# Both feed-forward products of an encoder block by Strassen's seven block products

## The chip, the cores and the metric

One core of a Trainium2 chip runs the whole program. The metric is the device time of one execution in microseconds; three runs of the kernel before took 2787.19, 2792.93 and 2794.11 us. TensorE (PE) multiplies, PEld is its weight load; VectorE (DVE), ScalarE (ACT) and GpSimd (POOL) work on elements; SyncE (SP) and POOL issue DMAs.

## The reference

An encoder block on x of 2048 tokens and width 1024, all float32. Two branches (a gated MLP that mixes tokens in chunks of 128, and neighbourhood attention) are merged by sigmoid gates and projected; then comes the part that the change touches:

```
x  = x + merged @ w_out                                    # 1024 x 1024
h2 = rms_norm(x, norm2_g)                                  # per token
x  = x + square(relu(h2 @ w_ff1)) @ w_ff2                  # 1024 -> 4096 -> 1024
```

The norm's factor of a token is positive and constant over the width, so both kernels multiply by it after the first product.

## The kernel before

Everything is held transposed: tiles have 128 features on the partitions and 512 tokens along the free axis. Each float32 operand is split into a rounded part (hi, an ACT copy to float32r) and what that leaves (lo, a DVE subtraction that reads both from SBUF); a product of a 128x128 weight tile and a 128x512 activation tile is three matmuls, hi hi, hi lo and lo hi (`gemm`, line 141). `split` (lines 108 and 109) does it for weights.

The program computes the input projections for both halves of 1024 tokens, then attention with the gates' products in between (line 600 on), then for each half `merge` for two blocks of 512 tokens (line 646), `out_proj` (line 677) and `ffn` (line 694). `merge` loads both branches (`load_y`, line 633, issued by POOL), gates and weights, multiplies, and leaves 8 tiles of merged features in parts in SBUF. `out_proj` adds the product to x (line 688), makes the scaled parts of the norm's input (lines 256 and 257) and the sums of squares.

`ffn` takes 256 columns of w_ff1 at a time, 16 chunks. `up` gives for each of two column tiles and two token blocks one accumulation group of 8 x 3 matmuls, then relu times the norm's factor (DVE, line 703), square (ACT, line 704) and the split into parts (lines 706 and 707), which stay in SBUF. `down` multiplies two such rows by 256 rows of w_ff2: for each of 8 output tiles and two token blocks 2 x 3 matmuls, added to x by DVE from the PSUM bank (line 717). `down` of a chunk is written ahead of `up` of the chunk two later.

SBUF is cut into slots of 4 KB per partition: 5 for raw weights, 12 for their parts, 29 for activations. PSUM has 8 banks of 128x512: 3 for products ("mm"), 2 for scores ("s"), 2 for transposes and one more. Dependencies and semaphores are set by a tile framework. It also orders each engine's instructions: a planner goes through them with expected durations, and an engine takes the first in the text that is ready by then. On the chip each engine keeps to the order planned. `keep_in_program_order` pins an instruction behind the one before it in the text.

Of the kernel before, what the change touches and what calls it, by code (L numbers as in the profile page):

```python
# [32 lines left out]
NRAW, NW, NACT = 5, 12, 29  # L33
# [4 lines left out]
# Queries go in tiles of 8 rows and 16 columns. First key row and key rows of a block of query rows;  # L38
# first key column, key columns and kind of bias table of a block of query columns.
# [18 lines left out]

class Block:
    """The encoder block; one method for each part of it."""  # L60

    def __init__(self, ctx, tc, a):
        self.tc, self.nc, self.a = tc, tc.nc, a
        self.waiting = []
        pool = lambda name, bufs, **k: ctx.enter_context(tc.tile_pool(name=name, bufs=bufs, **k))
        self.slots = pool("slots", 1)
        self.half = pool("half", 5)
# [4 lines left out]
        self.ybp = pool("ybp", 1)  # L72
# [26 lines left out]
    def split(self, shape, src, name, pool=False):  # L99
        """float32 tile -> its float32r part and what that leaves, which is a float32r too."""  # L100
# [11 lines left out]
    def load_raw(self, w, c0, ncol, nkt, name):  # L112
        """Columns c0.. of a weight, all of its rows."""
# [8 lines left out]
    def split_w(self, raws, name, pool=False):  # L122
        """A function (kt, part) -> [128, columns]."""
# [12 lines left out]
    def gemm(self, out, pairs):  # L136
        """pairs: (stationary parts, moving parts) along the contraction."""
# [6 lines left out]
    def later(self, fn, n=1):  # L144
        """fn's instructions come after the next n products', so that TensorE needn't wait for their inputs."""
# [10 lines left out]
    def rsqrt(self, r, m, n):  # L156
        """r = m ** -0.5, the square root's table refined by a Newton step."""
# [85 lines left out]
    def load_x(self, tok):  # L243
        """x transposed, 512 tokens: [kt] -> [128, 512]."""
# [8 lines left out]
    def parts(self, x, g, name):  # L253
        """x times the norm's gain, in parts."""
# [5 lines left out]
    def squares(self, acc, x, first):  # L260
        """acc: sums of squares over the rows of x tiles, by partition."""
# [8 lines left out]
    def rms(self, acc, n=1):  # L270
        """Each token's factor of the RMS norm: a column for each 128 tokens, and along the free axis on all
        partitions. To come after the next n + 1 products."""
# [3 lines left out]
        def columns():  # L276
# [7 lines left out]
            b = self.h512(name="rs_b").rearrange("p (t q) -> p t q", t=4)  # L284
            nc.vector.tensor_copy(b, col.rearrange("p (t o) -> p t o", o=1).broadcast_to([P, 4, P]))
            self.later(lambda: turn(b))

        def turn(b):
# [3 lines left out]
            self.nc.scalar.copy(row, pt)  # L292

# [3 lines left out]
    def norm(self, xs, n):  # L297
        """The RMS norm's factors of 512 tokens."""
# [6 lines left out]
    def tok_gemm(self, w, hT, t):  # L305
        """[128 tokens of tile t, 512 columns]"""
# [5 lines left out]
    def feat_gemm(self, w, m, X, nk=8):  # L312
        """[128 columns (the m-th of w), 512 tokens]"""
# [60 lines left out]
    def mix(self, h, t, v, uT):  # L374
        """Mixes a chunk's tokens and multiplies by u."""
# [101 lines left out]
    def att_load(self, pair, rb):  # L477
        """Keys (parts on the two partition halves), queries (doubled) and values of 8 rows of queries."""
# [29 lines left out]
    def att_queries(self, unit):  # L508
        """The queries, a tile's after another's."""
# [12 lines left out]
    def att_scores(self, unit, bias, cb):  # L522
        """Softmax of two heads' scores."""
# [59 lines left out]
    def att_out(self, po, o, c2):  # L583
        """Two column blocks' outputs, in parts and in the tokens' order."""
# [48 lines left out]
    def load_y(self, src, tok):  # L633
        ys = []
        for k in range(4):
            t = self.slot([2, 512], F32R, "y")
            self.nc.gpsimd.dma_start(t, src[:, :, k, tok : tok + 512])
            ys.append(t)
        return ys

    def load_gates(self, tok, m):
        g = self.slot([2, 512], F32, "gates")
        self.nc.sync.dma_start(g, self.gt.rearrange("(i m p) t -> m p i t", i=2, p=P)[m, :, :, tok : tok + 512])
        return g

    def merge(self, tok, out):
        """out: the merged branches, transposed and in parts; in pieces to be called in turn."""
        nc, a = self.nc, self.a
        load = lambda c: [self.load_wk(a[n][0], c * 256, 256, 4, n) for n in ("w_o_a", "w_o_b")] if c < 4 else None
# [5 lines left out]
        gs = [self.load_gates(tok, m) for m in range(2)]  # L655
        for c in range(4):
            (wa, wb), nxt = nxt, load(c + 1)
            for mm in range(2):
                m = 2 * c + mm
                g = gs.pop(0)  # L660
# [5 lines left out]
                pa = self.feat_gemm(wa, mm, ya, 4)  # L666
                pb = self.feat_gemm(wb, mm, yb, 4)
# [3 lines left out]
                o = self.slot([2, 512], F32R, "mg")  # L671
                nc.scalar.copy(o[:, 0], g[:, 0])
                nc.vector.tensor_tensor(o[:, 1], g[:, 0], o[:, 0].bitcast(F32), ALU.subtract)
                out.append(o)
                yield

    def out_proj(self, x1, mg):
        """Adds to x1, and its norm: parts and factors."""
        a = self.a
        h2T = []  # L680
        acc = self.h512(name="acc")
# [143 lines left out]
```

## Time and profile before

| | |
|---|---|
| median of three runs | 2792.93 us (2787.19 to 2794.11) |
| span of the profiled execution | 2789.8 us |
| PE busy | 2755.4 us (99%), 12996 matmuls |
| DVE, ACT, POOL busy | 1441.9, 791.2, 177.2 us |
| DMA | 327.30 MB, mean 117 GB/s |

The page of the profile gives the span of the profiled execution, from its first instruction to its last, and no time of its own for what lies around that; the median of the runs stands 3.1 us above the span. A row of a group of instructions reads: line, engine, operation, tile written <- tiles read, shapes, count | busy us, mean ns of one | idle us of the engine before them <- what ended that. Matmuls are pipelined, so a matmul's mean length (389 ns) is longer than the distance from one to the next.

### The profile page before, as it was taken

What the parts mean: (1) busy time and instruction counts of PE and PEld (TensorE: products, weight loads), DVE (VectorE), ACT (ScalarE), POOL (GpSimd) and SP (SyncE); (2) the same over time, 40 slices, a digit from 0 to 9 for tenths busy, and PEclk for the clock granted to TensorE, in tenths of its full rate; (3) what the DMA queues carried; (4) which work ended last, traced back from release to release, by engine and by line L of the source; (5) the groups of instructions that cost most, each with busy time, mean ns of one, the idle gap of its engine ahead of it and who ended that gap; (6) DMA issues with size and microseconds to landing.
All of it is one profiled execution on the core that took longest, in us unless ns stands there. A gap on an engine that the chain in (4) does not pass through costs nothing.

```text
span 2789.8 us, 33783 instructions
## 1 busy us (share of the span) xinstructions
PE 2755.4 (99%) x12996; PEld 2262.3 (81%) x12996; DVE 1441.9 (52%) x2604; ACT 791.2 (28%) x1336; POOL 177.2 (6%) x232
## 2 busy tenths in 40 slices
PE   8999999999999999999999999999999999999999
PEld 7888888887777777888888888887788888888887
DVE  6555225556656576545445444455654445454454
ACT  6333225232333342432222212222442211212111
POOL 0006500002212100000000000000000000000000
PEclk9999999999999999999999999999999999999999
DMA  6458832456888886421111111147631111111101
GB/s 189 116 134 219 242 107 71 135 134 176 226 233 230 235 271 223 146 81 46 46 46 46 61 46 46 46 129 234 202 102 59 46 46 46 54 53 46 46 23 61
DMA packets 262225, 327.30 MB, mean 117 GB/s; under 512 B 24429, under 2 KB 177428, under 8 KB 262064
## 3 DMA queue, kind: packets, MB, share of 16 engines
q1 hardware_dynamic: 239072, 280.53, 33.9%
q0 software_dynamic: 21952, 44.60, 5.9%
q8 instruction: 103, 1.69, 0.3%
q14 instruction: 58, 0.48, 0.1%
q10 hardware_dynamic: 1040, 0.00, 0.0%
HBM read 245.77 MB, written 79.25 MB: 117 GB/s over the span
## 4 chain that ended last, share of the span: by engine, by line
PE 94%; DVE 3%; DMA 2%; ACT 1%; issue 1%; SPq 0%; DVEq 0%; ACTq 0%
PE fg L141 76%; PE tg L141 11%; PE pv L575 2%; PE pTp L562 2%; PE s L533 2%; DMA gates<-gt 1%; PE mix L379 1%; DVE p L549 0%; PE qT L420 0%; DMA wg<-in_w_in_dram 0%; DVE acc L268 0%; PE ms L280 0%; DMA w_o_a<-in_w_o_a_dram 0%; DMA wk<-in_w_in_dram 0%; DVE p L540 0%
## 5 line engine op out<-in xcount | busy, mean ns | idle before, releaser
L141 PE MATMUL fg<-h2T,w_hi 128*128 128x512 f32 x2048 | 630.9, 389 | 0.0
L141 PE MATMUL fg<-aT,w_hi 128*128 128x512 f32 x2048 | 630.8, 389 | 0.0
L717 DVE TENSOR_TENSOR x<-fg,x 128x512 f32<-128x512 f32 x512 | 353.4, 690 | 251.1 <-PE fg L141 250.1
L141 PEld LDWEIGHTS fg<-aT,w_hi 128*128 128x128 f32 x2048 | 384.4, 188 | 80.5 <-DVE aT L707 0.7
L141 PEld LDWEIGHTS fg<-h2T,w_hi 128*128 128x128 f32 x2048 | 384.1, 188 | 79.6
L141 PE MATMUL fg<-h2T,w_lo 128*128 128x512 f32 x1024 | 398.4, 389 | 0.0
L141 PE MATMUL fg<-aT,w_lo 128*128 128x512 f32 x1024 | 398.4, 389 | 0.0
L141 PE MATMUL fg<-hT,wg_hi 128*128 128x512 f32 x1024 | 330.2, 398 | 0.0
L703 DVE SCALAR_TENSOR_TENSOR relu<-fg,rs_row 128x512 f32<-128x512 f32 x128 | 88.5, 691 | 305.1 <-PE fg L141 305.1
L108 ACT CAST w_hi<-w 128x1024 fp32r<-128x1024 f32 x128 | 134.1, 1052 | 343.9 <-PE fg L141 343.9
L141 PEld LDWEIGHTS fg<-hT,wg_hi 128*128 128x128 f32 x1024 | 191.5, 189 | 44.3 <-issue 7.4
L141 PEld LDWEIGHTS fg<-h2T,w_lo 128*128 128x128 f32 x1024 | 192.2, 188 | 40.0
L141 PEld LDWEIGHTS fg<-aT,w_lo 128*128 128x128 f32 x1024 | 192.2, 188 | 39.8
L141 PE MATMUL fg<-hT,wg_lo 128*128 128x512 f32 x512 | 202.7, 396 | 0.0
L109 DVE TENSOR_TENSOR w_lo<-w,w_hi 128x1024 fp32r<-128x1024 f32 x128 | 156.0, 1221 | 87.7 <-ACT w_hi L108 87.6
L704 ACT ACTIVATE relu<-relu 128x512 f32<-128x512 f32 x128 | 80.8, 631 | 420.6 <-DVE relu L703 420.6
L141 PE MATMUL fg<-mg,wo_hi 128*128 128x512 f32 x512 | 158.1, 390 | 0.0
L706 ACT CAST aT<-relu 128x512 fp32r<-128x512 f32 x128 | 79.5, 621 | 252.2 <-PE fg L141 249.1
L462 DVE TENSOR_TENSOR g<-fg,rs_row 128x512 f32<-128x512 f32 x64 | 44.1, 690 | 177.6 <-PE fg L141 174.2
L707 DVE TENSOR_TENSOR aT<-relu,aT 128x512 fp32r<-128x512 f32 x128 | 88.1, 688 | 76.8 <-ACT aT L706 76.8
L543 ACT ACTIVATE p<-p,nmx 128x480 f32<-128x480 f32 (+5 forms) x128 | 76.6, 600 | 149.8 <-DVE nmx L540 149.2
L141 PEld LDWEIGHTS fg<-hT,wg_lo 128*128 128x128 f32 x512 | 96.8, 189 | 19.7 <-issue 1.0
(166 smaller groups left out, 3525.0 us busy)
## 6 DMA issues: line engine op xcount, KB each, us to landing
w<-in_w_ff_dram SPq DMA_DIRECT2D x128, 512.0 KB
x<-in_xT_dram SPq DMA_DIRECT2D x32, 512.0 KB
wg<-in_w_in_dram SPq DMA_DIRECT2D x32, 512.0 KB
gt<-g SPq DMA_DIRECT2D x64, 256.0 KB
qn<-qs SPq DMA_DIRECT2D x64, 256.0 KB
gates<-gt SPq DMA_DIRECT2D x32, 512.0 KB
wo<-in_w_out_dram SPq DMA_DIRECT2D x32, 512.0 KB
ya<-ya SPq DMA_DIRECT2D x16, 512.0 KB
```

The source lines that it names most:

```text
L108: nc.scalar.copy(hi, src)
L109: nc.vector.tensor_tensor(lo, src, hi.bitcast(F32), ALU.subtract)
L141: self.nc.tensor.matmul(out, w[p], x[q], start=(i == 0 and j == 0), stop=(i == n - 1 and j == 2))
L533: nc.tensor.matmul(s.rearrange("p (r k) -> p r k", k=w), qt[hd][:, cb, l, :], kt[hd][:, :, k0 : k0 + w], start=(l == 0), stop=(l == 1),)
L543: nc.scalar.activation(p[:, hd], p[:, hd], AF.Exp, bias=nmx[:, hd : hd + 1], scale=-1.0, accum_out=sums[:, hd : hd + 1])
L562: nc.tensor.transpose(tp[: r * w, j // per, :], p[:, hd, j * w : (j + r) * w], self.ident)
L575: self.nc.tensor.matmul(po[hd * HD : (hd + 1) * HD, cb % 2 * P : (cb % 2 + 1) * P], unit[3][cb // 2][:m, cb % 2, j // per, hd * HD : (hd + ...
L703: nc.vector.scalar_tensor_tensor(r, pt, 0.0, rs[b][1], ALU.max, ALU.mult)
L704: nc.scalar.activation(r, r, AF.Square)
L706: nc.scalar.copy(o[:, 0], r)
L707: nc.vector.tensor_tensor(o[:, 1], r, o[:, 0].bitcast(F32), ALU.subtract)
L717: nc.vector.tensor_tensor(x, pt, x, ALU.add)
```

## The change

The feed-forward of a half is computed on 1024 tokens at once, and both its products as 2x2 blocks: two tiles of 128 columns by two blocks of 512 tokens by pairs of contraction tiles. In Winograd's form of Strassen's method four block sums on each side go in, seven block products are made instead of eight, and their sums come out. The sums over PSUM are partly made by letting a product go on accumulating in a bank after an earlier product in it has been read out.

POOL makes the four block sums of weights (`w_prep`) and of activations (`x_prep`); ACT and DVE then split each into parts. relu's squared result is stored whole to DRAM (`af`) and loaded again for the second product. There the contraction is visited in sliding groups: a visit (j, lo, hi) adds row pairs lo to hi-1 to output pair j; the 19 visits of a half have 1, 2, 3, then thirteen times 4, then 3, 2, 1 row pairs, so that each loaded pair serves four visits in a row and is then dropped. Preparation for the next step (`jobs`) is written between the seven products of the present one.

SBUF is shared out anew for the second part: 51 buffers of 4 KB that are taken from and given back to a list, on the memory of the old pools; a new buffer waits only for the tiles that it lies on. In the first half the merged tiles are stored to DRAM (`mg`) and loaded again. `load_y` issues from SP there. The attention and the input projections keep their code; comments and docstrings are gone.

```diff
+    def second_part(self):
+        self.part.close()
+        self.second = True
+        self.more = self.ctx.enter_context(self.tc.tile_pool(name="more", bufs=1, reuse_waits="tile"))
+        self.free = list(range(NBUF))
+    def take(self, shape, dt=F32, name="buf"):
+        i = self.free.pop(0)
+        return i, self.more.tile([P] + shape, dt, tag=f"b{i}", name=name)
...
+                if not self.second:
+                    nc.sync.dma_start(self.mg[tok // 512, m], o.bitcast(F32))
...
+    def w_prep(self, o):
+        n = o["n"]
+        r1, r2 = o["r1"][1], o["r2"][1]
+        o["t23"] = self.take([n, 2, P], F32, "w_s23")
+        s23 = o["t23"][1]
+        self.sub(s23[:, :, 1], r1[:, :, 0], r1[:, :, 1])
+        self.nc.gpsimd.tensor_tensor(r1[:, :, 1], r1[:, :, 1], r2[:, :, 1], ALU.add)
+        yield
+        o["t4"] = self.take([n, P], F32, "w_s4")
+        self.sub(s23[:, :, 0], r1[:, :, 1], r1[:, :, 0])
+        self.sub(o["t4"][1], r2[:, :, 0], s23[:, :, 0])
+        yield
+        self.parts_of(o, "r1", [n, 2, P])
+        yield
+        self.parts_of(o, "t23", [n, 2, P])
+        yield
+        self.parts_of_one(o, "t4", [n, P])
+        self.parts_of(o, "r2", [n, 2, P])
...
+    def x_prep(self, o):
+        r1, r2 = o["r1"][1], o["r2"][1]
+        o["t23"] = self.take([2, 512], F32, "x_t23")
+        t23 = o["t23"][1]
+        self.sub(t23[:, 1], r2[:, 1], r1[:, 1])
+        self.sub(r1[:, 1], r1[:, 1], r1[:, 0])
+        yield
+        o["t4"] = self.take([512], F32, "x_t4")
+        self.sub(t23[:, 0], r2[:, 1], r1[:, 1])
+        self.sub(o["t4"][1], r2[:, 0], t23[:, 0])
+        yield
...
+    def seven(self, w, xs, evac, jobs, done=()):
+        nc = self.nc
+        n = len(xs)
+        z, x, y = self.ps("z", "mm"), None, None
+        for i, p in enumerate((1, 5, 6, 3, 7, 2, 4)):
+            if p == 5:
+                x = self.ps("x", "s")
+            elif p == 2:
+                y = self.ps("y", "s")
+            out = {5: x, 3: x, 2: y}.get(p, z)
+            (wn, wi), (xn, xi) = self.W_AT[p], self.X_AT[p]
+            for k in range(n):
...
+                for j, (u, v) in enumerate(((0, 0), (0, 1), (1, 0))):
+                    nc.tensor.matmul(out, a[u], b[v], start=(p in (1, 5, 2) and k == 0 and j == 0), stop=(k == n - 1 and j == 2),
+                                     skip_group_check=p in (6, 3, 7, 4))
+            self.flush()
...
+            evac[p](out)
+            for _ in range(-(-len(jobs) // (7 - i))):
+                jobs.pop(0)()
...
+        def up_evac(c):
...
+            def finish(n, i, src):
+                t, v = e[n]
+                r = rs[i][1]
+                nc.vector.scalar_tensor_tensor(v[:, i], src, 0.0, r, ALU.max, ALU.mult)
+                nc.scalar.activation(v[:, i], v[:, i], AF.Square)
+                e[n, i] = True
+                if (n, 1 - i) in e:
+                    nc.sync.dma_start(self.af[2 * c + n, :, tok : tok + 1024].rearrange("p (b t) -> p b t", b=2), v)
+                    self.give(t)
...
+            return {1: copy(0, 0), 5: copy(1, 1), 6: copy(0, 1), 3: add(0, 1), 7: add(1, 1), 2: add(0, 0),
+                    4: lambda bank: finish(1, 0, bank)}
+        def down_evac(j):
...
+            return {1: add((0, 0)), 5: add((1, 1)), 6: add((0, 1)), 3: add((0, 1)), 7: add((1, 1)), 2: add((0, 0)), 4: add((1, 0))}
...
+        for c in range(NU):
+            nw = wl1(c + 1) if c + 1 < NU else wl2(0)
+            jobs = self.pieces(self.w_prep(nw))
+            self.seven(w, xs, up_evac(c), jobs, xs if c == NU - 1 else ())
+            w = nw
...
+        for j in x_new(0):
+            j()
+        for v, (j, lo, hi) in enumerate(visits):
...
+            self.seven(w, [win[k] for k in range(lo, hi)], down_evac(j), jobs, done)
```

In `seven`, `a` and `b` are the two parts of the weight and activation blocks that the product uses. Each add of `down_evac`, and the first operation of each add of `up_evac`, is a DVE addition of a PSUM bank to a tile in SBUF; `parts_of` is one ACT copy and one DVE subtraction of a whole 128x1024 buffer, `parts_of_one` of 128x512, `sub` a POOL subtraction. In `out_proj` the row pairs of x are scaled by ACT and prepared by `x_prep` in the second block's steps (`h2_jobs`).

## Rows read from the trace of the kernel before

**Rows 1.** The page: span, busy time by engine, granted clock in 40 slices.

```profile
span 2789.8 us, 33783 instructions
PE 2755.4 (99%) x12996; PEld 2262.3 (81%) x12996; DVE 1441.9 (52%) x2604; ACT 791.2 (28%) x1336; POOL 177.2 (6%) x232
PEclk9999999999999999999999999999999999999999
```

**Rows 2.** Chain of waits, its longest pieces: start us, us, what.

```profile
1217.26 685.69 PE fg L141 x3024
...
2100.28 685.69 PE fg L141 x3024
```

**Rows 3.** Stretches: length, then engines' busy us, clock, DMA share, GB/s.

```profile
core 0: us, PE busy (x) PEld busy (x) DVE busy (x) ACT busy (x) POOL busy (x), PEclk, DMA share, GB/s
1000.00:1080.80 80.80, 78.85 (x447) 62.78 (x445) 60.47 (x135) 34.52 (x71) 5.61 (x8) 1.00 0.87 268
...
1217.30:1902.90 685.60, 685.60 (x3025) 567.43 (x3024) 329.42 (x443) 146.34 (x197) 5.89 (x9) 1.00 0.20 62
1902.90:1963.90 61.00, 54.66 (x230) 44.34 (x228) 34.25 (x45) 21.92 (x31) 5.28 (x8) 0.94 0.73 225
```

**Rows 4.** Groups by line, whole span.

```profile
L717 DVE TENSOR_TENSOR x<-fg,x 128x512 f32<-128x512 f32 x512 | 353.4, 690 | 251.1 <-PE fg L141 250.1
...
L109 DVE TENSOR_TENSOR w_lo<-w,w_hi 128x1024 fp32r<-128x1024 f32 x128 | 156.0, 1221 | 87.7 <-ACT w_hi L108 87.6
L108 ACT CAST w_hi<-w 128x1024 fp32r<-128x1024 f32 x128 | 134.1, 1052 | 343.9 <-PE fg L141 343.9
...
L707 DVE TENSOR_TENSOR aT<-relu,aT 128x512 fp32r<-128x512 f32 x128 | 88.1, 688 | 76.8 <-ACT aT L706 76.8
...
L704 ACT ACTIVATE relu<-relu 128x512 f32<-128x512 f32 x128 | 80.8, 631 | 420.6 <-DVE relu L703 420.6
...
L706 ACT CAST aT<-relu 128x512 fp32r<-128x512 f32 x128 | 79.5, 621 | 252.2 <-PE fg L141 249.1
...
L106 POOL TENSOR_TENSOR wg_lo<-wg,wg_hi 128x1024 fp32r<-128x1024 f32 x16 | 38.4, 2398 | 50.2 <-PE tg L141 38.0 <-PE fg L141 9.1 <-POOL wg_hi L105 1.7
...
L256 ACT ACTIVATE h2T<-x,g 128x512 fp32r<-128x512 f32 x32 | 23.1, 723 | 77.5 <-DVE x L688 52.0 <-PE fg L141 18.8 <-issue 6.7
```

**Rows 5.** Timeline of POOL, its shorter additions: start us, us, instruction.

```profile
232.07 0.96 POOL L218 TENSOR_TENSOR tbt<-tbt,cmask 128x360 f32<-128x360 f32 x1 [0.70 <-DMA tbt<-sk]
...
268.80 2.10 POOL L218 TENSOR_TENSOR tbt<-tbt,cmask 128x480 f32<-128x480 f32 x1 [1.76 <-DMA tbt<-sk]
```

**Rows 6.** Timeline of POOL, 657 to 666 us.

```profile
658.79 2.37 POOL L106 TENSOR_TENSOR wg_lo<-wg,wg_hi 128x1024 fp32r<-128x1024 f32 x1
661.11 1.03 POOL L105 CAST wg_hi<-wg 128x1024 fp32r<-128x1024 f32 x1
...
664.50 1.04 POOL L105 CAST wg_hi<-wg 128x1024 fp32r<-128x1024 f32 x1
```

**Rows 7.** Timeline of DVE in the same stretch.

```profile
658.98 2.21 DVE L165 TENSOR_SCALAR rsq_t<-rsq_t 128x8 f32<-128x8 f32 x1
661.22 0.94 DVE L166 TENSOR_TENSOR qrs<-qrs,rsq_t 128x8 f32<-128x8 f32 x1
...
664.62 0.69 DVE L408 TENSOR_TENSOR qn<-tg,qrs 128x512 f32<-128x512 f32 x1
```

**Rows 8.** Timeline of DVE around 269 us.

```profile
268.59 1.22 DVE L109 TENSOR_TENSOR wg_lo<-wg,wg_hi 128x1024 fp32r<-128x1024 f32 x1 [2.89 <-ACT wg_hi L108]
```

**Rows 9.** Timeline of SP's queue at the end of the first half.

```profile
1861.98 1.52 SPq L643 DMA_DIRECT2D gates<-gt  x3
...
1885.40 18.62 SPq L720 DMA_DIRECT2D out_dram<-x  x15
```

**Rows 10.** The y tiles' DMAs, from issue to landing.

```profile
DMA to landing us min/median/max: 4.1/6.7/10.9
```

**Rows 11.** Chain of waits, its last piece: start us, us, what.

```profile
2785.99 0.69 DVE x L717
```

More of the change, by code (lines that the diff above doesn't have):

```diff
@@ L83, in __init__, with first_part, give, new @@
         self.tb = [[d(f"tb{i}{j}", [NH, 8, 16, n * w]) for j, n in enumerate(KIND_N)] for i, w in enumerate(KIND_W)]
+        self.af = d("af", [FF // P, P, S])
+        self.mg = d("mg", [2, 8, P, 2, 512])
+    def first_part(self):
+        part = ExitStack()
+        pool = lambda name, bufs: part.enter_context(self.tc.tile_pool(name=name, bufs=bufs, reuse_waits="tile"))
+        self.slots = pool("slots", 1)
+        self.half = pool("half", 5)
+        self.ybp = pool("ybp", 1)
+        self.part = part
+    def second_part(self):
[6 more added lines that the diff above has]
+        return i, self.more.tile([P] + shape, dt, tag=f"b{i}", name=name)
+    def give(self, *ts):
+        self.free += [t for t in ts if t is not None]
+    def new(self, shape, dt, name, tag="act"):
+        return self.take(shape, dt, name) if self.second else (None, self.slot(shape, dt, name, tag))
     def slot(self, shape, dt=F32, name="slot", tag="act"):
@@ new lines, in pieces, with load_out @@
+    @staticmethod
+    def pieces(gen, n=5):
+        return [lambda: next(gen, None)] * n
+    def load_out(self, c):
+        own, ts = [], []
+        for r in range(2):
+            raw, rv = self.take([4, 256], F32, "wo")
+            src = self.a["w_out"][0][r * 512 : (r + 1) * 512, c * 256 : (c + 1) * 256]
+            self.nc.sync.dma_start(rv, src.rearrange("(k p) n -> p k n", p=P))
+            hi, lo = self.take([4, 256], F32R, "wo_hi"), self.take([4, 256], F32R, "wo_lo")
+            self.hilo(hi[1], lo[1], rv)
+            self.give(raw)
+            own += [hi[0], lo[0]]
+            ts.append((hi[1], lo[1]))
+        return own, lambda kt, hl: ts[kt // 4][hl][:, kt % 4]
@@ new lines, in load_merged, with out_proj @@
+    def load_merged(self, b):
+        out = []
+        for m in range(8):
+            t, v = self.take([2, 512], F32R, "mg")
+            self.nc.sync.dma_start(v.bitcast(F32), self.mg[b, m])
+            out.append((t, v))
+        return out
+    def out_proj(self, tok, mgs):
+        nc, a = self.nc, self.a
+        self.x1 = [self.take([2, 512], F32, "x1") for _ in range(8)]
+        for m in range(8):
+            nc.sync.dma_start(self.x1[m][1].rearrange("p b t -> p (b t)"), a["xT"][m * P : (m + 1) * P, tok : tok + 1024])
+        x1 = [x[1] for x in self.x1]
+        acc = self.take([2, 512], F32, "acc")
+        sq = self.take([2, 512], F32, "sq")
+        rs, xs, jobs = [], [], []
+        steps = [(b, c) for b in range(2) for c in range(4)]
+        nxt = self.load_out(0)
+        if not mgs:
+            mgs = [self.load_merged(0)]
+        for i, (b, c) in enumerate(steps):
+            (own, w), nxt = nxt, self.load_out(steps[i + 1][1]) if i < 7 else None
+            if i == 1 and len(mgs) < 2:
+                mgs.append(self.load_merged(1))
+            for mm in range(2):
+                m = 2 * c + mm
+                pt = self.feat_gemm(w, mm, [v for _, v in mgs[b]])
+                x = x1[m][:, b]
+                nc.vector.tensor_tensor(x, pt, x, ALU.add)
+                if m == 0:
+                    self.tc.keep_in_program_order(nc.scalar.activation(acc[1][:, b], x, AF.Square))
+                else:
+                    nc.scalar.activation(sq[1][:, m % 2], x, AF.Square)
+                    nc.vector.tensor_tensor(acc[1][:, b], acc[1][:, b], sq[1][:, m % 2], ALU.add)
+                for _ in range(min(3, len(jobs))):
+                    jobs.pop(0)()
+            self.give(*own)
+            if c == 3:
+                rs.append(self.rms(acc[1][:, b], 1))
+                self.give(*(t for t, _ in mgs[b]))
+            if b == 1:
+                jobs += self.h2_jobs(x1, c, xs)
+        self.give(sq[0])
+        for j in jobs:
+            j()
+        return xs, rs, acc[0]
```

261 lines of the change are left out of this document (176 added, 85 removed).

## The prediction

> **What bounds the kernel now.** I read the busy times first: TensorE (PE) is busy 2755.4 us of a span of 2789.8, VectorE (DVE) 1441.9, ScalarE (ACT) 791.2, GpSimd (POOL) 177.2, at a granted clock of nine tenths or more in all slices [rows 1]. Then the chain of waits: its two longest pieces are the two feed-forward halves, each 3024 matmuls in 685.69 us with nothing between them [rows 2], so 0.22675 us per 512-column matmul. The table of stretches says the same: PE busy 685.60 of 685.60 us there, DVE 329 (48%), the DMA engines 20%; only where a merge begins does the DMA come near its limit, 268 GB/s at a share of 0.87, and PE stands 2 to 6 us [rows 3]. So time goes with the number of matmuls, as long as nothing else fills up. The page's span is 2789.8 us and the median of the three runs 2792.93; the 3.1 us outside the span are added at the end as a constant.
>
> **What it removes.** Up, a chunk of 256 columns and 1024 tokens took 4 groups of 8 x 3 matmuls, 96; it now takes 7 block products of 4 x 3, 84, so 1344 per half instead of 1536. Down, a visit of n row pairs takes 7 x 3n = 21n, and the n of a half sum to 64: again 1344 instead of 1536. Per half 2688 instead of 3072; 768 matmuls fewer in all, 768 x 0.22675 = **174.1 us off** the path, since PE has no gaps to absorb it.
>
> **What it adds on the other engines.** A full up step and a full down visit (n = 4) now last 84 x 0.22675 = 19.05 us on PE. Per operand set, weights or activations, there are four POOL additions of 128x512 and four splits, three of 128x1024 and one of 128x512, each an ACT copy and a DVE subtraction. DVE: 3 x 1.221 + 0.688 = 4.35 us; ACT: 3 x 1.052 + 0.621 = 3.78 [rows 4]. A POOL addition of 512 elements is not in the trace; between 360 elements at 0.96 us [rows 5] and 1024 at 2.398 [rows 4] a straight line gives 1.29 us, so 5.2 per set (bounds 1.0 and 2.4 each).
> Up step: DVE 4.35 + 7 evictions x 0.69 = 9.2 of 19.05, ACT 3.78 + 3 copies + 4 squares at 0.63 = 8.2, POOL 5.2. All lie beside PE. A product that accumulates on a bank (third, fourth, fifth, seventh) waits for an eviction of 0.69 us while a whole other product (12 matmuls, 2.7 us) runs: covered. I take 0.1 us per step for 32 steps, **+3** (bounds 0 and 32).
> Down visit: two sets per visit, so DVE 8.7 + 7 x 0.69 = 13.5 (71%), ACT 7.6, POOL 10.3, DMA 2.1 MB, half of what the 268 GB/s of rows 3 move. relu's result adds 16.8 MB out and 16.8 in per half, 54 GB/s over some 620 us. Taken one by one every engine is hidden. Taken together they are not, and that is the main point of this forecast.
>
> **The port.** While POOL ran an addition of 2.37 us (658.79 to 661.16) [rows 6], an 8-element DVE instruction begun at 658.98 took 2.21 us, and a two-input one of 8 elements begun at 661.22 took 0.94, to the end of the POOL cast of 661.11 [rows 7]. In the other direction a POOL addition of 480 elements took 2.10 us where the line above gives 1.22: it began at 268.80, inside a DVE subtraction that ran from 268.59 to 269.81 [rows 5, 8]. So such pairs exclude each other for their whole length. But the DVE multiplication from PSUM at 664.62 took its usual 0.69 us inside the next POOL cast [rows 7]. The Trainium skill (GPSIMD Engine Reference, Specifications) says that the SBUF interfaces are shared with VectorE, with contention for DVE instructions in a 2-port mode or with two SBUF inputs; by that the splits are held and the evictions, which read a PSUM bank, are not, as these rows show on small instructions. By the rule a visit needs 19.0 us of the port, without it 13.5 of DVE, and the sum below would lose its two largest terms.
> From the rows: splits 8.7 + additions 10.3 = **19.0 us of exclusive work in a visit of 19.05**. The port becomes as full as PE, with two in-order queues on it. Nothing is lost if both always have work ready; if DVE stood for every addition, it would need 13.5 + 10.3 = 23.8. I take one addition's length, 1.29 us, per full visit, as a held split delays the eviction behind it in DVE's queue, and the product two places later waits for that bank. There are 12 such visits per half (the thirteenth prepares no activations): 24 x 1.29 = **+31** (bounds 0 and 24 x 4.75 = 114).
>
> **The ramp.** The first three visits of a half have n = 1, 2, 3: 126 matmuls, 28.6 us on PE. Before the fourth, four activation sets and weights of n = 1 to 4 must be prepared: 4 x (5.2 + 4.35) = 38.0, POOL 13.9 for the weights, splits 11.8 (the same lines at 128 to 512 elements), 63.7 us of port. The last up step leaves 19.05 - (4.35 + 3 x 0.69 + 5.2) = 7.5, and 5 us of it is due only inside the fourth visit. Left uncovered: 63.7 - 28.6 - 7.5 - 5 = 22.6 per half, **+46** for two (bounds 2 x 10, when loads come early enough for more of it to lie in the up steps, and 2 x 45, when DVE and POOL alternate and the first load waits for the last store). Here idle PE may also lose its clock: in the stretch with 6.3 us of idle time the granted clock was 0.94 of full, 7.3 us at the half level, worth up to 3.7 us [rows 3]; that is inside the bounds.
>
> **From output projection to up.** The last row pair is complete only at the end of the projection: eviction 0.69, scaling 1.05 to 1.45, two additions 2.6, copy 1.05, subtraction 1.22 [rows 4]: 6.8 us, against some 2.5 us of matmuls on the other three pairs and the norm's; 4.3 stand open, with 3.7 for the clock 8 per half, **+16** (bounds 4 and 24).
>
> **Starts of the halves.** First half: merged tiles go out to DRAM and come back (4.2 MB each way before the projection can finish a column), and the new buffers lie on the old pools' memory. At 268 GB/s [rows 3] the 8.4 MB are 31 us in a stretch whose DMA is full; the way back, 16 us, I count in full, **+16** (bounds 3, if merge matmuls hide it, and 35: x1, first weights and merged tiles, 9.4 MB, all after the last merge product). Second half: the y loads move from POOL's queue into SP's, with stores and weights ahead of them. The order there isn't that of the text: three gate loads at 1861.98 stand ahead of the fifteen stores from 1885.40 [rows 9], so part goes out early. One y load took 6.7 us to land [rows 10]. **+4** (bounds -6, the present idle gone, and +20: 5.2 MB at 268 GB/s). Within each merge, the mixed order and the weights are as before.
>
> **Tail.** The last visit has 4.76 us of PE against 7 evictions, 4.83, and the last store is 512 KB instead of 256; the final addition ends 3.1 us before the span does now [rows 1, 11]: **+3** (bounds 1 and 6).
>
> **Sum.** -174.1 + 3 + 31 + 46 + 16 + 16 + 4 + 3 = -55; 2789.8 - 55 + 3.1 = **2738 us**. With all lower bounds -152 (2641), with all upper +147 (2940).
>
> **Rivals.**
> A. *The port is no bound*: POOL's additions fall where DVE waits for PE, as 250.1 us of DVE's idle time before the present evictions is waiting for PE [rows 4]. Visits cost nothing, the ramp 20: losses 62, so 2681 us. Against it: 19.0 of 19.05 leaves no room for queueing.
> B. *DVE and POOL take turns*: each full visit takes 23.8 us because splits wait for additions and evictions wait behind splits; 114 + 90 for the ramp + 42 for the other terms = 246, **slower, 2865 us**. It decides from 22.6 us per full visit, (174 - 88)/24 = 3.6 over PE's 19.05, with the ramp as forecast. For it: rows 7, where DVE got through only between POOL instructions. Against it: evictions are not held, and 5.5 us of a visit DVE has nothing to do.
> C. *The transfers decide*: both starts at their upper bounds (35 and 20) and the projections at 24, everything else as forecast: losses 162, 2781 us, hardly any change. For it: DMA share 0.87 already. Against: planned order with early loads.
> D. *It does not do what it says*: the matmuls are fewer but slower than 0.22675, as accumulating groups wait for evictions in visits of n = 1 and 2, where a product is 0.7 to 1.4 us. Five such visits per half, at most 12 us in all beyond the ramp: 2750; it changes no sign.
>
> **Chances.** Forecast 0.41 (own range 2700 to 2775), A 0.27, B 0.15, C 0.14, D 0.03. Differences below 0.3%, 8 us, can't be told from none here. Faster: forecast, A, D and some of C, 0.75; same, from C, 0.06; slower, B and the rest of C, 0.19. The range takes in A and most of C and stops short of B: 2650 to 2830.
>
> **What will show it.** 5376 matmuls in the seven products, at a start-to-start of 0.227 in a full up step, which must last 19 to 19.2 us. In a full down visit I expect 20 to 21 us, DVE splits of 2 us and more wherever a POOL addition runs, and PE's idle time there put down to DVE. If splits keep 1.22 us beside additions, the port was wrong. Visits 0 to 2 should take about 50 us instead of 28.6, mostly waiting for DVE and POOL; a gap of 4 to 8 us should stand ahead of each first up step, and about 16 ahead of the first projection with DMA as the releaser. A full visit at 22.6 us or more would make the forecast wrong in sign; 19.1 would make it A.

## The result and the profile after

The changed kernel takes 2859.09 us (median; 2855.48 to 2865.75) against 2792.58 of the kernel before, a ratio of 1.0243 (95% interval 1.0228 to 1.0259). It is slower, where 2738 and faster were forecast. The page of the kernel after, span, busy times and granted clock, against [rows 1]:

```profile
span 2853.0 us, 33593 instructions
PE 2653.3 (93%) x12228; PEld 2154.5 (76%) x12228; DVE 1584.5 (56%) x2606; ACT 1008.8 (35%) x1600; POOL 776.1 (27%) x656
PEclk9999999999999998989999999999999999999999
```

The 768 matmuls are gone (12996 to 12228), PE's busy time fell by 102 us, and its share from 99% to 93%: PE now waits for some 200 us. The stretches of the first half, columns as in [rows 3] (start of the up steps, up steps, first visits, full down visits):

```profile
1231.00:1268.00 37.00, 18.77 (x68) 14.75 (x68) 24.37 (x25) 16.87 (x22) 19.77 (x13) 0.72 0.15 43
1275.00:1540.00 265.00, 265.00 (x1171) 219.41 (x1169) 126.02 (x154) 106.59 (x153) 74.59 (x59) 1.00 0.33 109
1564.40:1606.30 41.90, 33.66 (x128) 25.23 (x127) 41.70 (x43) 18.57 (x23) 33.65 (x20) 0.92 0.32 109
1606.30:1902.80 296.50, 253.06 (x1010) 203.59 (x1009) 170.62 (x184) 85.30 (x96) 136.21 (x97) 0.92 0.27 88
```

In the up steps PE is as full as in [rows 3]. In the full visits it is idle for 43 of 296.5 us at a granted clock of 0.92, yet DVE is busy only 58% of the time, POOL 46% and DMA 27%: no engine is full there. From the first matmul of each step to that of the next, the span's 63.2 us (2853.0 - 2789.8) fall to these places, against the terms of the forecast:

| place | measured | forecast |
|---|---|---|
| 768 matmuls fewer, at 0.22675 us each | -174.1 | -174.1 |
| 24 full down visits (24.7 and 24.4 us each, 19.05 of matmuls) | **+131.8** | +31 |
| output projection to up: 18.2 us without a product in each half, the first projection itself 4.0 longer, first up steps 26.3 and 24.7 | **+52.8** | +16 |
| ramp: first three visits 41.8 and 44.3 for 28.6, last up steps 23.3 and 21.6 | +35.8 | +46 |
| first product of the first output projection later | +21.5 | +16 |
| up steps 2 to 15, 19.04 us each | 0 | +3 |
| end visits, tail, start of the second half (the rest) | -4.6 | +7 |

What a full visit waits for is seen by setting one of PE's waits beside the other engines' queues. Timeline of PE, DVE, ACT and POOL of the kernel after (start us, us, instruction, idle time before it and what ended it):

```profile
1739.94 0.39 PE L838 MATMUL x<-r_hi,t_hl 128*128 128x512 f32 x1
1744.08 0.75 PE L838 MATMUL z<-t_hi 128*128 128x512 f32 x1 [3.75 <-DVE x L1000]
1744.63 0.63 PE L838 MATMUL z<-t_lo,t_hi 128*128 128x512 f32 x1
1745.06 0.63 PE L838 MATMUL z<-t_hi,t_lo 128*128 128x512 f32 x1
...
1747.60 0.40 PE L838 MATMUL z<-t_hi,t_lo 128*128 128x512 f32 x1
...
1732.21 0.69 DVE L1000 TENSOR_TENSOR x<-z,x 128x512 f32<-128x512 f32 x1 [2.03 <-PE z L838]
1734.93 0.69 DVE L1000 TENSOR_TENSOR x<-x,x 128x512 f32<-128x512 f32 x1 [2.03 <-PE x L838]
1739.88 1.35 DVE L746 TENSOR_TENSOR r_lo<-a_r,r_hi 128x1024 fp32r<-128x1024 f32 x1 [4.25 <-ACT r_hi L745]
1741.15 2.28 DVE L746 TENSOR_TENSOR r_lo<-w_r,r_hi 128x1024 fp32r<-128x1024 f32 x1
1743.35 0.68 DVE L1000 TENSOR_TENSOR x<-z,x 128x512 f32<-128x512 f32 x1
...
1738.79 1.05 ACT L745 CAST r_hi<-a_r 128x1024 fp32r<-128x1024 f32 x1 [13.34 <-POOL a_r L742]
...
1732.11 1.29 POOL L782 TENSOR_TENSOR w_r<-w_r,w_r 128x512 f32<-128x512 f32 x1 [1.28 <-DMA w_r<-in_w_ff_dram]
...
1737.47 1.29 POOL L742 TENSOR_TENSOR a_r<-a_r 128x512 f32<-128x512 f32 x1
...
1740.22 2.12 POOL L742 TENSOR_TENSOR x_t<-a_r,x_t 128x512 f32<-128x512 f32 x1
```

Read it from below. POOL makes the sums for the next visit one behind the other, 1.29 us each, so `a_r` is done at 1738.8. On DVE the splits of `a_r` and `w_r` stand ahead of the eviction of `z` (the matmul after the last one into `z` started at 1737.45). DVE idles 4.25 us at the head of its queue for `a_r`, then splits for 3.5 us, one of them held by the POOL addition of 1740.22, and only then evicts. In the text of `seven` this eviction comes first; the instruction order that was planned for DVE has it behind. An eviction that nothing holds starts 0.43 us after its last matmul has started (so in e2 below), which would be at 1737.65 here. It starts 5.7 us later: 2.2 us are DVE's idle time, 3.5 us the two splits, of which the hold makes about 1.1 (2.28 for 1.22). The product in between covers part of that. PE waits 3.75 us, and its next matmuls then start 0.43 us apart instead of 0.227, until 1747.60, at a granted clock of 0.52. Together 19.05 + 3.75 + 1.6 = 24.4 us. The waits of DVE and of PE in the full visits of the first half (us in total, times, longest):

```profile
DVE r_lo L746 <- ACT r_hi L745: 53.9, 14, 6.5
...
PE z L838 <- DVE x L1000: 39.6, 11, 4.0
```

Between output projection and up the same engines meet again. POOL, DVE and PE of the kernel after, second half:

```profile
2136.40 1.27 POOL L742 TENSOR_TENSOR x_t<-h_r,h_r 128x512 f32<-128x512 f32 x1 [4.89 <-ACT h_r L926]
...
2138.97 2.24 POOL L742 TENSOR_TENSOR w_s<-w_r 128x512 f32<-128x512 f32 x1
2141.17 2.24 POOL L742 TENSOR_TENSOR x_t<-h_r,h_r 128x512 f32<-128x512 f32 x1
...
2144.60 2.27 POOL L742 TENSOR_TENSOR x_t<-h_r,x_t 128x512 f32<-128x512 f32 x1
...
2138.24 4.05 DVE L746 TENSOR_TENSOR r_lo<-h_r,r_hi 128x1024 fp32r<-128x1024 f32 x2
...
2148.57 2.30 DVE L746 TENSOR_TENSOR r_lo<-w_r,r_hi 128x1024 fp32r<-128x1024 f32 x1
...
2148.52 0.80 PE L838 MATMUL z<-r_hi 128*128 128x512 f32 x1 [10.52 <-ACT r_hi L745]
```

The last output projection matmul started at 2130.3, the first up product at 2148.5. The first weights' sums stand among those of the last row pair on POOL, and additions of 1.29 us take 2.2 beside splits, splits of 1.22 us take 2.0 to 2.3 beside additions. This is the exclusion of [rows 6 to 8] on whole tiles, in both directions; the eviction of 1732.21, which reads a PSUM bank, took its usual 0.69 us inside the POOL addition of 1732.11. With the rule that the prediction quotes (the Trainium skill, GPSIMD Engine Reference, Specifications: contention for DVE instructions with two SBUF inputs) these rows agree: splits, which have two, are held, the eviction is not.

### The profile page after: what moved, and what is told of

The parts are those of the page before. It is cut to its first block, busy times and chain, and to the rows that moved or that the text cites. A ratio compares the mean times of both kernels' runs of the same rounds, so it can differ in the third digit from the quotient of the medians.

```text
span 2853.0 us, 33593 instructions
## 1 busy us (share of the span) xinstructions
PE 2653.3 (93%) x12228; PEld 2154.5 (76%) x12228; DVE 1584.5 (56%) x2606; ACT 1008.8 (35%) x1600; POOL 776.1 (27%) x656
## 4 chain that ended last, share of the span: by engine, by line
PE 71%; DVE 8%; DMA 6%; POOL 6%; issue 5%; ACT 2%; SPq 0%; POOLq 0%; DVEq 0%; ACTq 0%
PE fg L170 24%; PE z L838 18%; PE tg L170 11%; PE x L838 7%; PE y L838 4%; DMA w_r<-in_w_ff_dram 4%; DVE r_lo L746 3%; PE pv L608 2%; POOL x_t L742 2%; POOL w_s L742 2%; PE s L566 2%; PE pTp L595 2%; DVE x L1000 1%; POOL a_r L742 1%; POOL w_r L782 1%
## 5 line engine op out<-in xcount | busy, mean ns | idle before, releaser
L742 POOL TENSOR_TENSOR w_s<-w_r 128x512 f32<-128x512 f32 (+3 forms) x140 | 176.4, 1260 | 741.4 <-DMA w_r<-in_w_ff_dram 376.0
L838 PE MATMUL z<-t_hi 128*128 128x512 f32 x512 | 219.7, 429 | 79.5 <-DVE x L1000 79.4
L746 DVE TENSOR_TENSOR r_lo<-w_r,r_hi 128x1024 fp32r<-128x1024 f32 (+3 forms) x140 | 189.1, 1353 | 181.4 <-DMA af<-relu 142.4
L838 PE MATMUL z<-t_lo,t_hi 128*128 128x512 f32 x512 | 215.8, 422 | 0.0
L838 PE MATMUL z<-t_hi,t_lo 128*128 128x512 f32 x512 | 215.1, 420 | 0.0
L745 ACT CAST r_hi<-w_r 128x1024 fp32r<-128x1024 f32 (+3 forms) x140 | 136.5, 975 | 197.8 <-POOL w_r L782 130.3
L838 PEld LDWEIGHTS z<-t_hi 128*128 128x128 f32 x512 | 105.5, 206 | 114.7 <-DVE x L1000 89.9
L170 PE MATMUL fg<-mg,wo_hi 128*128 128x512 f32 x512 | 159.7, 394 | 22.2 <-DMA mg<-mg 22.2
L838 PE MATMUL x<-r_hi,t_hl 128*128 128x512 f32 x512 | 171.2, 393 | 6.9 <-DVE x L1000 6.9
L838 PE MATMUL z<-t_hl,r_hi 128*128 128x512 f32 x512 | 160.8, 396 | 12.0 <-DVE x L1000 7.2
L170 PEld LDWEIGHTS fg<-mg,wo_hi 128*128 128x128 f32 x512 | 97.0, 190 | 42.7 <-ACT wo_hi L745 22.6
L838 PEld LDWEIGHTS z<-t_hi,t_lo 128*128 128x128 f32 x512 | 105.9, 207 | 24.1
```

What stands on the lines that cost most here:

```text
L170: self.nc.tensor.matmul(out, w[p], x[q], start=(i == 0 and j == 0), stop=(i == n - 1 and j == 2))
L742: self.nc.gpsimd.tensor_tensor(out, x, y, ALU.subtract)
L745: self.nc.scalar.copy(hi, x)
L746: self.nc.vector.tensor_tensor(lo, x, hi.bitcast(F32), ALU.subtract)
L838: nc.tensor.matmul(out, a[u], b[v], start=(p in (1, 5, 2) and k == 0 and j == 0), stop=(k == n - 1 and j == 2), skip_group_check=p in (6, ...
```

## Experiments

Three theories at first. L: the loads of the down visits come late for want of a buffer. Q: splits stand ahead of evictions in DVE's queue. P: the port, POOL's additions and DVE's splits holding each other. Times are of one run each, unless an interval is given, so a difference under some 8 us (0.3%) is read from the steps in the traces and not from the time; the kernel before took 2791 to 2796 us beside them. "Gap" is the time without a product ahead of the first up step.

**e1, one buffer more.**

```diff
-NRAW, NW, NACT, NBUF = 5, 12, 29, 51
+NRAW, NW, NACT, NBUF = 5, 12, 29, 52
-    ... dynamic_dma_scratch_size=8192)
+    ... dynamic_dma_scratch_size=4096)
```

> One SBUF buffer more (52 instead of 51). The changed kernel's full down visits take 24.4 us instead of 19.05. Theory L (loads late): a visit's two weight loads wait for buffers that the end of the visit before gives back, then come 5.3 us of DMA and six POOL additions before a split that PE's next product waits behind. With one buffer more each load goes out one release earlier, 1 to 2 us, so visits of 22.5 to 23.5 us and some 2825 us in all. Theory Q (order on DVE): the eviction of the third product is queued behind two splits, whatever the loads do; the splits come earlier with the data, so the same 22.5 to 23.5, or nothing if the splits are held by POOL. Theory P (port): exclusive work is 19.0 us as before, so 24.4 and 2859 us.

2893.03 us, 34 slower, which none of the theories had; full visits 25.7 and 25.5. The planned order differs again: on DVE's timeline of e1 the eviction of `z` stands behind a split that waits 2.91 us and one that is held.

```profile
1804.91 1.34 DVE L746 TENSOR_TENSOR r_lo<-a_r,r_hi 128x1024 fp32r<-128x1024 f32 x1 [2.91 <-ACT r_hi L745]
1806.18 2.28 DVE L746 TENSOR_TENSOR t_lo<-w_s,t_hi 128x1024 fp32r<-128x1024 f32 x1
1808.39 0.68 DVE L1000 TENSOR_TENSOR x<-z,x 128x512 f32<-128x512 f32 x1
```

L is not borne out: more room did not help. It is not refuted here either, as the order changed along with the room; e2, whose visits are short with the same 51 buffers, speaks against it as the one cause.

**e2, splits of the down visits pinned.** They keep their place in the text on DVE, behind the evictions; the additions stay on POOL.

```diff
-        self.nc.vector.tensor_tensor(lo, x, hi.bitcast(F32), ALU.subtract)
+        ins = self.nc.vector.tensor_tensor(lo, x, hi.bitcast(F32), ALU.subtract)
+        if self.down:
+            self.tc.keep_in_program_order(ins)
```

> In the down visits each split's DVE subtraction is pinned behind what stands before it in the text, so that the eviction of the third product goes ahead of the splits that are written after it. Theory Q: PE's 3.75 us wait for that eviction and the slow clock after it (1.5 us) go, visits of 19.1 to 20.5 us, some 2740 to 2765 us in all. Theory L: the splits are as late as before and the next eviction waits behind them instead, visits of 22 to 24.4 us, 2810 to 2860. Theory P: no change, 24.4 and 2859 us, since the exclusive work is the same.

2752.85 us, 106 less; full visits 19.74 and 19.75. The first half's full visits of e2:

```profile
1615.10:1851.90 236.80, 232.53 (x1008) 188.25 (x1009) 165.13 (x182) 86.32 (x97) 147.17 (x96) 1.00 0.32 105
```

One of its visits on DVE's timeline:

```profile
1747.11 1.34 DVE L747 TENSOR_TENSOR r_lo<-a_r,r_hi 128x1024 fp32r<-128x1024 f32 x1 [2.27 <-ACT r_hi L746]
1748.37 0.68 DVE L1003 TENSOR_TENSOR x<-x,x 128x512 f32<-128x512 f32 x1
1748.97 1.72 DVE L747 TENSOR_TENSOR t_lo<-w_s,t_hi 128x1024 fp32r<-128x1024 f32 x1
```

The split still waits 2.27 us for POOL's chain, and splits are still held (1.72), but none stands ahead of the third product's eviction any more (one or two ahead of others, as here of the fourth's), and the clock stays at 1.00. Q holds for the visits; P is worth no more than 19.74 - 19.05 = 0.7 us per visit once the order is right. The price: the ramp is 50 us here, 42 to 44 before, of which the last up steps, back at 19.04, return 4.2 and 2.6; the gap is 18.2 as it was.

**e3, additions of the down visits on DVE** (in `sub`, and likewise the addition in `w_prep`; order as planned).

```diff
-        self.nc.gpsimd.tensor_tensor(out, x, y, ALU.subtract)
+        (self.nc.vector if self.down else self.nc.gpsimd).tensor_tensor(out, x, y, ALU.subtract)
```

> In the down visits the eight additions of a visit run on DVE instead of POOL, 0.69 us each instead of 1.29; DVE's own work is then 19.0 us of a visit of 19.05. Theory P: nothing is held any more, splits go back to 1.22 us, but DVE is full: 20 to 21 us per visit, about 2760 us. Theory L: the chain from the loads to the split is 4 us shorter, 20.5 to 22 us. Theory Q: eight more instructions stand in front of evictions in the same queue: 24 us or more, 2850 to 2900 us.

2724.5 us; full visits 19.33 and 19.38, ramp 42.0 and 42.2. So the down visits mend by either cure. Q as it stood expected 24 us or more here: it counted the instructions in front of the evictions and not what they wait for. Ahead of the third product's eviction DVE is idle for 0.2 us per full visit on the mean here, 4.0 in the changed kernel.

**e4, additions of the down visits left out** (the second product's block sums are not made; `no_adds` takes the same buffers and makes the same splits, of the tiles as loaded).

```diff
     def x_prep(self, o):
+        if self.down:
+            yield from self.no_adds(o, [2, 512], [512])
+            return
```

`w_prep` likewise.

> The down visits leave out their block additions (the splits take the loaded tiles instead, so the second product is not the reference's); loads, splits, buffers and matmuls are the same in number. POOL is idle there. Theories L and P both: the chain is 10 us shorter and nothing holds the port, visits of 19.05 to 19.5 us, about 2735 us. Theory Q: the order on DVE is planned anew, and if splits stay ahead of an eviction some wait remains, 20 us or more.

2698.63 us; full visits 19.14, ramp 31.9 and 34.5. The floor: splits and evictions alone cost a visit 0.1 us, and the ramp still 3 to 6. The three theories are not parted by it: the additions take their hold and their chain along, and the new plan puts one split ahead of that eviction instead of two.

**e5, first weights earlier** (on e3): the first w_ff1 block is loaded and prepared within the projection's last step, and the second norm's column sums are issued before the last splits.

```diff
+            if i == 7:
+                w1 = self.w_load(a["w_ff1"][0], [0, 2, 4, 6], [1, 3, 5, 7], 0)
+                jobs += self.pieces(self.w_prep(w1), 6)
...
+                if b == 1:
+                    self.flush()
```

> Built on the kernel with the down visits' additions on DVE (2724.5 us); two edits at the end of the output projection: the first w_ff1 block is loaded and prepared during its last step, and the column sums of the second normalisation are issued before the last pair's splits. If the 18.2 us without a matmul between the output projection and the first up step, and the 7 us that this step is longer than the others, come from the weights' preparation being emitted last, the gap falls to 8 us or less and the first step to 20 us: 10 to 16 us per half, 2724 to 2695-2705. If they come from the last pair alone (scale, additions, splits of x), both stay within 2 us: 2722 to 2726.

2714.86. The gap fell to 5.3, but the first step rose from 26.3 to 32 and the second by 1.1 to 1.4: some 6 us per half, between the two expectations.

**e6, mg's loads first** (on e3).

```diff
-        for m in range(8):
-            nc.sync.dma_start(self.x1[m][1]...)
         ...
         if not mgs:
             mgs = [self.load_merged(0)]
+        for m in range(8):
+            nc.sync.dma_start(self.x1[m][1]...)
```

> Built on the kernel with the down visits' additions on DVE (2724.5 us); w_out's and mg's loads of the first half are issued ahead of the eight loads of x1. If the queue's order made the first product late by 21.5 us (x loads ahead of mg's, at a DMA share of 1.00), the first product comes 5 to 10 us earlier: 2714 to 2720. If the volume of all loads together sets it, or the first eviction then waits for x1, it is unchanged: 2723 to 2726.

2720.54. The first product came 11.2 us earlier, the last one of that projection only 1.9 us earlier. PE's waits in e6 (the kernel after had one, 22.2 us for `mg`, and 1.0 for a split of w_out), and the chain of e6 ahead of the second:

```profile
PE fg L171 <- DMA mg<-mg: 10.8, 1, 10.8
PE fg L171 <- ACT wo_hi L746: 9.2, 1, 9.2
...
1130.75 10.22 DMA x<-in_xT_dram
...
1141.04 10.43 DMA wo<-in_w_out_dram
...
1151.57 1.05 ACT wo_hi L746
```

The order set when the first product starts, but most of the wait only changed its name: the next block of w_out now comes behind x1's loads. Whether a third order would save more, or the volume of the transfers sets the rest, no run shows.

**e7, e3 and e2 together.**

```diff
+        if self.down:
+            self.tc.keep_in_program_order(lo)
```

> Built on the kernel with the down visits' additions on DVE (2724.5 us, full visit 19.35); the splits of the down visits keep their place in the text on DVE too. Order on DVE's queue as the one cause: with both edits a full visit has nothing left to gain, 19.1 to 19.4, and only the ramp can move (42 us, 35 to 50): 2710 to 2735. Port as a second cause beside the order: the same, since neither kernel has additions on POOL in these visits, so this run sets no verdict between them; it says whether the two cures add up (they would give 2640 if they did: 106 + 135 us off 2859 less the 15 that they share with nothing).

2717.08, full visits 19.04 and 19.08, the length of their matmuls.

**e8, e5, e6 and e7 together.**

> Additions of the down visits on DVE, splits of the down visits in the text's order, the first w_ff1 block prepared within the output projection, mg's loads ahead of x1's. If the stages are independent, the savings add: 2724 less 20 to 32 less 5 to 10, so 2682 to 2699. If one stage's time only moves to the next, 2705 to 2724.

2707.61, in the second range: the full visits are at 19.07, but gap and first step take 5.3 and 32 to 33 us, and the first projection takes 102 us where e7 has 92, so what was mended at the start was mostly lost in the stage behind it.

**e9, splits pinned in the projection and the up steps too** (on e8; `self.pin` set from `out_proj` on).

```diff
-        if self.down:
+        if self.pin:
```

> All of the last kernel's edits (2707.6 us), and the splits keep their place in the text in the output projection and the up steps too. In the last kernel 5.3 us lie between output projection and up step, and the first up step takes 32 to 33 us; its last two evictions of the output projection stand behind three to five splits on DVE (started 2058.2 and 2065.1, with the matmuls done at 2056). If DVE's order delays them, the first step falls to 24 to 28 us: 2692 to 2702. If the chain of eviction, scale, POOL additions and splits of the last pair sets it whatever the order, it stays at 30 to 33 and the time within 3 us of 2707.6.

2719.23: first step 29.1, but the gap 10.6 and the second projection 7.6 us longer. The text's order does not mend this stage. DVE's timeline of e9 shows a reason: in the text, too, splits stand ahead of the projection's last two evictions, and ahead of the first of these they are held.

```profile
2061.34 2.31 DVE L748 TENSOR_TENSOR r_lo<-h_r,r_hi 128x1024 fp32r<-128x1024 f32 x1
2063.57 2.31 DVE L748 TENSOR_TENSOR t_lo<-x_t,t_hi 128x1024 fp32r<-128x1024 f32 x1
2065.80 1.75 DVE L748 TENSOR_TENSOR t_hl<-x_t,t_hl 128x512 fp32r<-128x512 f32 x1
2067.47 2.28 DVE L748 TENSOR_TENSOR r_lo<-h_r,r_hi 128x1024 fp32r<-128x1024 f32 x1
2069.67 0.68 DVE L907 TENSOR_TENSOR x<-fg,x 128x512 f32<-128x512 f32 x1
```

These four splits take 8.65 us where [rows 4] make 4.35, without a gap on DVE. An order with those evictions first was not run.

**e10, first two row groups prepared in the last up step** (on e9).

```diff
+            if c == NU - 1:
+                jobs += x_late(0) + x_late(1)
```

> The same, and the first two groups of rows of the second product are loaded and prepared within the last up step instead of after it. If the ramp (42 us against 28.6 of matmuls, and 32 to 34 with the additions left out) is the time to prepare row groups in its short visits, it falls to 31 to 36 us, with the last up step at most 4 us longer: 6 to 11 us per half, 12 to 20 below the kernel before it. If the preparation of its weights sets the ramp, it stays above 39 us.

2726.52, ratio 0.9757 (0.9740 to 0.9773) to the kernel before, and no faster than e9: the ramp is 44 (43 in e9), the last up step 20.6 and 21.5.

**e11, first weights one step earlier still** (on e8: `i == 6`).

> The 2707.6 us kernel (all four edits), with the first w_ff1 block loaded and prepared one step of the output projection earlier. If what is left between output projection and up step (5.3 us without a matmul, and 13 to 14 us more in the first step) is work crowded into the last step, 6 to 10 us per half go: 2688 to 2696. If DVE has no free time in either step, the output projection lengthens by as much as the first step gains: 2704 to 2711.

2703.86: gap 0.2, first step 36.7; moved once more, not removed.

**e12, no addition left on POOL from the projection on** (on e8).

```diff
-        (self.nc.vector if self.down else self.nc.gpsimd).tensor_tensor(...)
+        (self.nc.vector if self.dve else self.nc.gpsimd).tensor_tensor(...)
     def out_proj(self, tok, mgs):
+        self.dve = True
```

> The 2707.6 us kernel with the block additions on DVE in the output projection and the up steps too, so none is left on POOL. With the splits pinned, DVE was busy without a gap in the last steps of the output projection, and its splits of x took 2.28 to 2.31 us beside POOL's additions against 1.22 alone. Held splits as the cause of the late first up step: four additions of 0.68 us on DVE are cheaper than four splits held for 1.1 us each, so 3 to 8 us per half go there, and the up steps stay at 19.04: 2690 to 2702. DVE full as the cause: the additions come on top of its work, the output projection and the first up step lengthen by 3 to 6 us per half: 2713 to 2720.

2683.62: gap 0.2, first step 24.1, 13 to 14 us less per half, and up steps of 19.04. Two stretches of e12, around the second half's first up step and its ramp:

```profile
2040.00:2070.00 30.00, 28.78 (x124) 22.84 (x123) 28.77 (x44) 20.04 (x27) 0.00 (x0) 0.94 0.16 39
...
2356.10:2398.10 42.00, 33.73 (x127) 23.64 (x126) 42.00 (x64) 18.89 (x25) 0.00 (x0) 0.96 0.34 113
```

The gain holds both the exclusion and the shorter addition (0.69 us on DVE, 1.29 on POOL); no run parts the two.

**e13, e12 with the row groups of e10.**

> The 2683.6 us kernel (no additions on POOL), with the first two row groups of the second product loaded and prepared within the last up step. In the ramp DVE was busy for 42.0 of 42 us, in the up steps for 0.6 of the time. If the ramp is DVE's work (its splits, additions and evictions), moving two groups of 7 to 8 us each into a step with 7 us to spare takes 7 to 14 us off per half and lengthens the last up step by 2 to 8: 2660 to 2680. If the ramp waits for the weights of its visits, it stays at 39 to 42: 2681 to 2690.

2682.83, no change. DVE got to group 0's sums at 2346.1, when its load had landed, 11 us into the last up step, and DVE is busy 41.4 of 42 us behind it: the edit moved too little to tell the two theories apart. Whether the ramp can be shortened stays open.

**e14, the changed kernel with one edit: all block additions on DVE.**

```diff
-        self.nc.gpsimd.tensor_tensor(out, x, y, ALU.subtract)
+        self.nc.vector.tensor_tensor(out, x, y, ALU.subtract)
...
-        self.nc.gpsimd.tensor_tensor(r1[:, :, 1], r1[:, :, 1], r2[:, :, 1], ALU.add)
+        self.nc.vector.tensor_tensor(r1[:, :, 1], r1[:, :, 1], r2[:, :, 1], ALU.add)
```

> The changed kernel (2859.1 us) with one edit: all block additions, in every stage, on DVE and not on POOL; order of the queue and of the emission as the planner has them. Held instructions (a POOL addition and a DVE split take turns) as what makes DVE late, both in the down visits (+131.8) and ahead of the up steps (+52.8): full visits 19.1 to 19.5, and gap and first up step together 10 to 20 us shorter per half: 2685 to 2710. Order of DVE's queue alone: it could as well stay at 24 us per full visit, 2800 to 2860; and with the first w_ff1 block still prepared last, gap and first step stay at 44 us, so 2715 to 2730 if only the down visits mend.

2705.76, 153 less than the changed kernel from two changed lines: full visits 19.5 and 19.4, gap 12.7 and 13.2, first step 21.5, ramp 42. The stretch of full visits of e14:

```profile
1597.00:1800.00 203.00, 200.25 (x876) 163.37 (x875) 187.04 (x248) 75.27 (x83) 0.00 (x0) 1.00 0.33 112
```

DVE is at 92% here, and PE waits less than with DVE at 58%. Three to four splits or additions on the mean still stand ahead of the third product's eviction, two before, but DVE is idle there for 0.4 us per visit instead of 4.0. The expectation laid a cure in both stages to the hold; but this edit takes away the hold, the longer addition and the chain on POOL at once, and in the visits e2 parts them: there the hold stayed, and 0.7 us with it.

**e15, e12 timed.**

> The 2683.6 us kernel again (additions on DVE from the output projection on, splits of the down visits pinned, the first w_ff1 block prepared within the output projection, mg's loads first), timed in rounds against the kernel before: 2680 to 2690 and a ratio of 0.959 to 0.963, if its one look was no outlier.

2682.17 us (2678.51 to 2682.84), ratio 0.9597 (0.9581 to 0.9613) to the kernel before: this version beats both.

## Why the prediction was wrong

*What it removes*: right, 5376 matmuls in the seven products, at 0.227 us in the up steps, and nothing lost there.

*The port, full visits*: this step failed, and the sign with it. "I take one addition's length, 1.29 us, per full visit, as a held split delays the eviction behind it": measured are 5.5 on the mean, 131.8 in all, above the upper bound of 114. The sizes under it were right (the POOL addition 1.29, splits held to 2.28, and with the order mended, e2, 0.7 us over PE's time where 1.29 was taken). What it left out is the order: it took every split to be ready when DVE reached it. In the planned order two splits stand ahead of an eviction, and the first waits at the head of DVE's queue for a chain that POOL has only begun (load at 1732, five additions, ACT's copy). So DVE stands idle with an eviction behind it that could go. The price is what is left of POOL's chain when the eviction is ready (2.2 us in the visit shown) and the splits behind it (3.5 us), less the product in between, not the length of one addition; and a slower clock behind each wait (1.6 us), which the step had not counted. Its own sign of being wrong, 22.6 us or more per full visit, came true. The upper bound failed by the same assumption: 4.75 us is work on two engines in turn, with no idle time in it. Two cures, the order (e2) and a shorter chain on the other engine (e3, e14), each remove nearly all of it, so in this kernel the loss needs both. Whether earlier loads in the same order would be a third cure, no run shows.

*Rival B* had the time (2865; 2859 measured) and the full visit (23.8; 24.4 to 24.7), and of its mechanism the half that evictions wait behind splits. That DVE and POOL alternate without rest is refuted by DVE's 58%. That its sum fits too is luck: it had 90 for the ramp (35.8 measured) and 42 for the other terms (70). *Rival A*, the port as no bound, is refuted by the held splits, in the full visits (2.28 us) as in e9; in the visits with the order mended (e2) it was nearly right. *Rival C*, the transfers: DMA is at 27% in the full visits, and the first start, 21.5, is below its 35. *Rival D*: the up steps' matmuls keep 0.227.

*From output projection to up*: +52.8 for +16, above its upper bound of 24. The step priced one row pair's chain with free engines (6.8 us). It did not count that the first weights are prepared in the same place, nor that sums and splits there hold each other (8.65 us for 4.35, e9). No engine is full there (DVE 24.4 of 37 us, POOL 19.8): PE waits for a chain, 10.5 us of it until ACT's copy behind POOL's sums. e5 and e11 show the first to be mostly a shift, e12 most of the rest together with the shorter additions.

*Ramp*: +35.8 for +46, right in kind (2 x 22.6 is 45); DVE is busy 41.7 of 41.9 us, held time included. *First start*: +21.5 for +16, with DMA as the releaser as said; e6 shows that the order of the loads sets half of it, but that the projection's end gains only 1.9 us by another order. *Up steps*: 0 for +3. *Tail and second start*, with the end visits: -4.6 for +7, not told apart.

## What to carry to other kernels

A balance of busy times per step says what an engine can do, not when: before costing a preparation at nothing, look at which in-order queue holds both it and the work that releases PE, and ask what the preparation itself waits for. A long producer chain on a slow engine ahead of a split costs what is left of it if a ready eviction stands behind the split, so keep evictions first or make the chain short. Moving cheap additions to the busier engine can be the faster choice when the two hold each other: DVE went from 58% to 92% and the kernel lost 153 us.

## What the runs showed of the hardware

- An addition of 512 elements on POOL takes 1.29 us alone and 2.1 to 2.3 beside a DVE split; the split takes 1.22 alone and 2.0 to 2.3 beside it. A DVE addition that reads a PSUM bank isn't held: all 266 of the down visits took at most 0.69 us. The block addition takes 0.69 us on DVE (e14).
- After PE's wait of 3.75 us matmuls start 0.43 us apart from 1744.08 to 1747.60, at a granted clock of 0.52, which is the lower of the two levels (1.2 of 2.4 GHz). Over the full visits the granted clock is 0.92; in those of e2, with waits of at most 1.6 us, it is 1.00.
